# A recurrent scan, half of it moved into the projection loop; convolutions on VectorE and parked in DRAM

## The chip, the cores and the metric

The kernel runs on one core of one Trainium2 chip. The metric is device time in microseconds (us) of one execution. Engines are named as the profile names them: PE (TensorE matmul), DVE (VectorE), ACT (ScalarE), POOL (GpSimd), SP (SyncE, which here only issues DMAs).

## The reference

Two blocks on 512 tokens of width 2048. The change lies in the first one:

```python
h = rms_norm(x, norm_mix) @ w_in            # conv value+gate, r, k, v, three low-rank inputs
u = val * sigmoid(gate)                     # 1024 channels
u = silu(layer_norm(depthwise_conv(u, 31 taps, causal) + bias))
# RWKV-7 mixing, 16 heads of 64:
S = S * w_t + (S @ a_t) b_t + v_t k_t       # 64x64 state per head, one step per token
y_t = S @ r_t                               # then group norm per head, bonus, gate
x = x + concat(u, y) @ w_out                # then the expert layer (32 experts, 2 per token)
```

The second block (windowed attention, a state-space layer and a merge) follows; nothing in it changes. All values are float32; a projection is made of three matmuls on values split into a high and a low part.

## The kernel before

All that changes is in `phase_a` (L169 on): norm, projections, convolutions, scan, output projection. Channels lie on 128 partitions, the 512 tokens along the free axis.

A projection of 128 channels is one `dense`: four chunks of four weight tiles. Each chunk is loaded over the SP queue (L103), split by ACT (`wh`, L47) and DVE (`wl`, L48), and used by 12 matmuls (L111 to L113) against the split input `uh`, `ul`. Three buffers of split weights lie between the two. There are 43 such projections: 3 low-rank, 24 for r, k, v (three for each of 8 *pairs* of heads) and 16 for the 8 convolutions (gate and value).

The pair loop (`for p in range(8)`) makes r, k, v of a pair, the cumulated decay (a scan along the tokens, L410), operands scaled by it (`arr`, L427 to L433), the 64x64 score blocks of 8 chunks of 64 tokens (`sc`, L460), and more operands (L473 to L482), and writes them to DRAM (`dS`, `dL`). After pair 3 and after the loop, `inverse(0)` and `inverse(1)` read `dL` of four pairs and invert all their triangular blocks: a chain of 62 small dependent DVE instructions (L349, L351), then matmuls and copies (L340 on), and a last write to DRAM (`dX`, `dO`, L362). The scan proper (from L500) loads the inverses of both halves into `XB` and walks the 8 chunks, the two halves of heads by turns; a chunk is five *blocks* of eight 64x64 matmuls each (L561, L572, L579, L586, L594; the first and last chunk have four) with copies by ACT and adds by DVE between, each depending on the one before. After each second chunk `finish` (L524 on) normalises.

A convolution is a gate (`conv_gate`, two projections) and 31 taps (`conv_taps`): on DVE one instruction a tap (L303, L311), on Pool an ACT product (L308) and a Pool add (L309). `CONV` says which convolutions are made in which pair's turn; `FILL` those made after the loop. Here 0, 2 and 4 are in the loop; 1, 3, 5, 6, 7 after it; the first five of 0, 1, 2, 3, 4 on Pool, the rest on DVE. When all eight exist, the layer norm (L619 to L632) runs and then `w_out(0)`, the first half of the output projection; `w_out(1)` needs the scan's end.

The framework's scheduler puts the instructions of each engine in one fixed order, in which each engine then runs them; an instruction that waits holds up all that stand behind it on its engine.

Of the kernel before, what the change touches and what calls it, by code (L numbers as in the profile page):

```python
# [167 lines left out]
def phase_a(k):  # L168
# [22 lines left out]
    dS = tc.dram_tile([8, 128, 8, 2, 4, 64], F32, name="dS")  # L191
# [91 lines left out]
    def conv_gate(p, bufs):  # L283
# [4 lines left out]
        nc.gpsimd.tensor_mul(sgm, sgm, R)  # L288
# [6 lines left out]
    def conv_taps(p, ug):  # L295
        o = VEC["conv_dw"][0] + 31 * p
        cv[p] = co.tile([128, T], F32, name="cv%d" % p)
        pool = p in POOL
        b = vec(k, "conv_b", p)
        if pool:  # L300
            nc.scalar.activation(cv[p], ug[:, 0:T], AF.Identity, scale=k.vec[:, o:o + 1], bias=b)
        else:
            nc.vector.tensor_scalar(cv[p], ug[:, 0:T], k.vec[:, o:o + 1], b, op0=OP.mult, op1=OP.add)  # L303
        for j in range(1, 31):
            w = k.vec[:, o + j:o + j + 1]
            if pool:
# [3 lines left out]
            else:  # L310
                nc.vector.scalar_tensor_tensor(cv[p], ug[:, j:j + T], w, cv[p], op0=OP.mult, op1=OP.add)  # L311
# [81 lines left out]
    for p in range(8):  # L393
# [5 lines left out]
        arr = rp.tile([128, 8, 4, 64], F32, name="arr")  # L399
# [61 lines left out]
        for h, sc in enumerate(scs):  # L461
# [4 lines left out]
            nc.sync.dma_start(dS[:, 0:64, p, h, 1].rearrange("c q t -> q c t"), sc[0:64, :, 1])  # L466
            nc.sync.dma_start(dS[:, 64:128, p, h, 0:2].rearrange("c q a t -> q c a t"), sc[64:128])
            for i, b in ((2, 0), (3, 3)):
                nc.sync.dma_start(dS[:, 0:64, p, h, b].rearrange("c q t -> q c t"), arr[hr, :, i])
        for c0 in range(0, 8, 4):  # L470
# [28 lines left out]
    for g in range(2):  # L499
        for h in range(2):  # L500
            for i in range(2):
                q = slice(h * 64 + i * 32, h * 64 + i * 32 + 32)
                nc.sync.dma_start(XB[q, g * 32:(g + 1) * 32, i * 32:(i + 1) * 32],
                                  dX[g][i, h * 32:(h + 1) * 32].rearrange("m s t -> s m t"))
            q = slice(h * 64, h * 64 + 32)
            for o in range(0, 32, 16):
                nc.sync.dma_start(XB[q, g * 32 + o:g * 32 + o + 16, 32:64], dO[g][2 * h + o // 16])
    bp = sctx.enter_context(tc.tile_pool(name="bd", bufs=2, side=RIGHT))
    yp_ = sctx.enter_context(tc.tile_pool(name="yr", bufs=2, side=RIGHT))
    pc2 = bp.tile([64, 8, 2, 8], F32, name="pc2", bufs=1)  # L510
    for h in range(2):
        nc.sync.dma_start(pc2[:, :, h], pc[h * 64:(h + 1) * 64])

    def chunk(cc, g):

        bd = bp.tile([128, 4, 2, 5, 64], F32, name="bd", bufs=4)
        g4 = slice(4 * g, 4 * g + 4)
        lo_, hi = slice(0, 64), slice(64, 128)
        nc.scalar.dma_start(bd[hi, :, :, 0:4], dS[cc, hi, g4])
        nc.scalar.dma_start(bd[lo_, :, :, 0:3], dS[cc, lo_, g4, :, 0:3])  # L520
        nc.scalar.dma_start(bd[lo_, :, :, 4], dS[cc, lo_, g4, :, 3])
        return bd

    def finish(y, t):  # L524

        ts = slice(t * 128, (t + 1) * 128)
        for q in range(2):
            g4 = slice(4 * q, 4 * q + 4)
            yp = y[:, g4]
            pm = psr.tile([128, 4, 128], F32, name="pr")  # L530
            nc.tensor.matmul(pm, k.blk, yp, start=True, stop=True)
            nc.vector.scalar_tensor_tensor(yp, pm, -1.0 / 64, yp, op0=OP.mult, op1=OP.add)
            sq = yp_.tile([128, 4, 128], F32, name="fsq", bufs=1)
            nc.scalar.activation(sq, yp, AF.Square)
            pv = psr.tile([128, 4, 128], F32, name="pr")
            nc.tensor.matmul(pv, k.blk, sq, start=True, stop=True)
            nc.vector.tensor_scalar(sq, pv, 1.0 / 64, 64e-5, op0=OP.mult, op1=OP.add)
            rs = rsqrt(k, tmp, sq, [128, 4, 128])
            nc.vector.tensor_mul(yp, yp, rs)
            gt = yp_.tile([128, 4, 128], F32, name="fgt", bufs=1)  # L540
            nc.scalar.dma_start(gt, dG[g4, :, ts].rearrange("a q t -> q a t"))
            bon = yp_.tile([128, 4, 128], F32, name="fbon", bufs=1)
            nc.scalar.dma_start(bon, dB[g4, :, ts].rearrange("a q t -> q a t"))
            nc.gpsimd.tensor_mul(yp, yp, gt)
            nc.gpsimd.tensor_add(yp, yp, bon)
            nc.sync.dma_start(dY[:, g4, ts], yp)

    cur = [chunk(0, g) for g in range(2)]
    for cc in range(8):
        if cc % 2 == 0:  # L550
            y = yp_.tile([128, 8, 128], F32, name="y")
        for g in range(2):
            g4 = slice(4 * g, 4 * g + 4)
            bd = cur[g]
            nxt = chunk(cc + 1, g) if cc < 7 else None
            kq = slice(0 if cc else 64, 128)
            pq = psr.tile([128, 2, 4, 64], F32, name="pr")
            ys = y[:, g4, (cc % 2) * 64:(cc % 2 + 1) * 64]
            for i in range(4):
                for h in range(2):  # L560
                    nc.tensor.matmul(pq[h * 64:(h + 1) * 64, 0, i], bd[kq, i, h, 0], bd[kq, i, h, 3], start=True,  # L561
                                     stop=True)
            qs = bp.tile([128, 4, 64], F32, name="qs")
            nc.scalar.activation(qs, pq[:, 0], AF.Copy)
            state = bd[0:64, :, :, 3]
            if nxt and cc:
                nc.vector.tensor_mul(nxt[0:64, :, :, 3], state,
                                     pc2[:, g4, :, cc:cc + 1].to_broadcast([64, 4, 2, 64]))
            if cc:
                for i in range(4):  # L570
                    for h in range(2):
                        nc.tensor.matmul(pq[h * 64:(h + 1) * 64, 1, i], bd[0:64, i, h, 3], bd[0:64, i, h, 4],  # L572
                                         start=True, stop=True)
                nc.scalar.activation(ys, pq[:, 1], AF.Copy)
            pu = [psr.tile([64, 4, 64], F32, name="pr") for _ in range(2)]
            for i in range(4):
                for h in range(2):
# [1000 lines left out]
```

## Time and profile before

| | us |
|---|---|
| median of 3 runs | 3401.13 (3394.83 to 3404.06) |
| the profiled execution | 3402.26 |
| its span, first to last instruction | 3400.6 |
| last projection matmul before the layer norm | 692.5 |
| first layer-norm instruction (L624) | 746.9 |
| first matmul of `w_out(0)` / of `w_out(1)` | 773.2 / 891.4 |
| end of `phase_a`'s projections, expert layer starts | about 1008 |

Over the whole span PE is busy 93%, DVE 49%, ACT 31%, POOL 16%, and the mean granted clock is 0.963. An engine's row of a timeline reads: start, duration, engine, line, operation, output and inputs, and in square brackets the idle time before it and what ended it.

### The profile page before, as it was taken

The page shows a single profiled execution, that of the slowest core. Times are in us where ns is not written, and L with a number is a line of the kernel's source. Part 1 is how long each engine was busy: PE and PEld are TensorE (multiplying, and loading weights), DVE is VectorE, ACT ScalarE, POOL GpSimd, SP SyncE. Part 2 cuts the span into 40 slices and gives each one's busy share as a digit, 9 for nine tenths or more (in the row PEclk, how much of TensorE's full clock was granted, in tenths as well). Part 3 has the DMA queues.
Part 4 walks back from the last instruction along what each step waited for, and adds up shares of the span by engine and source line. Part 5 has one row for each costly group of instructions (what it writes and reads, how often), then busy time and mean ns, then how long its engine had stood idle before and what let it go on. Part 6 is the DMA issues. An engine that isn't in the chain of part 4 may idle for free.

```text
span 3400.6 us, 41331 instructions
## 1 busy us (share of the span) xinstructions
PE 3171.8 (93%) x15156; PEld 2156.7 (63%) x15157; DVE 1658.1 (49%) x3072; ACT 1052.2 (31%) x1793; POOL 546.0 (16%) x581
## 2 busy tenths in 40 slices
PE   8999998779989899898999898999999999999999
PEld 6777666547664333333333346778777878888887
DVE  6666667993332222232223238445799443344433
ACT  6464564344330000000000024363322242353322
POOL 3052254543210000000000005372000100000000
PEclk9999999789999999899999998999999999999999
DMA  4445444767668999998999965435332653334343
GB/s 149 129 122 139 125 121 123 139 131 181 219 239 352 420 420 414 406 407 349 419 420 411 404 249 167 143 144 166 134 106 104 203 183 118 124 130 137 133 146 118
DMA packets 352495, 743.47 MB, mean 219 GB/s; under 512 B 110688, under 2 KB 176608, under 8 KB 302112
## 3 DMA queue, kind: packets, MB, share of 16 engines
q1 hardware_dynamic: 272576, 650.24, 52.1%
q10 hardware_dynamic: 70624, 60.52, 7.2%
q0 software_dynamic: 9088, 30.03, 2.7%
q8 instruction: 121, 1.98, 0.2%
q14 instruction: 86, 0.70, 0.1%
HBM read 674.96 MB, written 73.01 MB: 220 GB/s over the span
## 4 chain that ended last, share of the span: by engine, by line
PE 46%; DMA 4%; POOL 2%; DVE 1%; issue 1%; ACT 0%; ACTq 0%; SPq 0%; DVEq 0%; POOLq 0%
PE pd L113 10%; PE pd L111 10%; PE pd L112 10%; PE pgate L916 3%; PE py L937 3%; PE pup L916 2%; DMA xg<-dTok,ix 1%; DMA w<-expert_w_gate_dram 1%; PE pb L946 1%; PE pb L947 1%; PE pb L815 1%; PE pr L1345 1%; POOL cn L1115 1%; PE ps L1296 0%; POOL cm L1114 0%
## 5 line engine op out<-in xcount | busy, mean ns | idle before, releaser
L48 DVE TENSOR_TENSOR wl<-wraw,wh 128x512 fp32r<-128x512 f32 x636 | 478.0, 754 | 496.0 <-ACT wh L47 487.1
L47 ACT ACTIVATE wh<-wraw 128x512 fp32r<-128x512 f32 x668 | 418.0, 628 | 834.0 <-PE pd L112 677.7
L113 PE MATMUL pd<-u2h,wl 128*128 128x512 f32 x1088 | 437.7, 402 | 10.2 <-DVE wl L48 10.1
L111 PE MATMUL pd<-u2h,wh 128*128 128x512 f32 x1088 | 439.4, 404 | 6.4 <-ACT wh L47 6.4
L112 PE MATMUL pd<-u2l,wh 128*128 128x512 f32 x1088 | 436.6, 401 | 0.0
L113 PE MATMUL pd<-uh,wl 128*128 128x512 f32 x688 | 282.6, 411 | 42.8 <-DVE wl L48 42.8
L916 PE MATMUL pgate<-w,xT 128*64 128x512 f32 x1024 | 305.6, 615 | 15.7 <-DMA w<-expert_w_gate_dram 15.0
L916 PE MATMUL pup<-w,xT 128*64 128x512 f32 x1024 | 293.5, 595 | 0.0
L111 PE MATMUL pd<-uh,wh 128*128 128x512 f32 x688 | 278.7, 406 | 12.0 <-ACT uh L220 7.2
L112 PE MATMUL pd<-ul,wh 128*128 128x512 f32 x688 | 278.1, 404 | 5.0 <-DVE ul L221 5.0
L113 PEld LDWEIGHTS pd<-u2h,wl 128*128 128x128 f32 x1088 | 206.5, 190 | 63.7 <-DVE wl L48 14.0
L309 POOL TENSOR_TENSOR cv<-cv,tap 128x512 f32<-128x512 f32 x150 | 227.6, 1517 | 105.1 <-ACT tap L308 92.4
L111 PEld LDWEIGHTS pd<-u2h,wh 128*128 128x128 f32 x1088 | 206.9, 190 | 56.7 <-ACT wh L47 9.0
L937 PE MATMUL py<-w,hidT 128*64 128x512 f32 x1024 | 236.0, 599 | 2.9 <-ACT hidT L929 2.9
L112 PEld LDWEIGHTS pd<-u2l,wh 128*128 128x128 f32 x1088 | 206.9, 190 | 47.8 <-issue 1.1
L948 DVE TENSOR_TENSOR hT<-hT,pb 128x512 f32<-128x512 f32 x256 | 159.2, 681 | 148.9 <-PE pb L947 148.9
L941 DVE SCALAR_TENSOR_TENSOR yl<-py,info,yh 128x512 fp32r<-128x512 f32 x64 | 48.0, 750 | 311.1 <-ACT yh L940 311.1
L916 PEld LDWEIGHTS pgate<-w,xT 128*64 128x64 f32 x1024 | 87.5, 142 | 170.0 <-issue 157.4
L113 PEld LDWEIGHTS pd<-uh,wl 128*128 128x128 f32 x688 | 134.0, 195 | 82.8 <-DVE wl L48 53.7
L916 PEld LDWEIGHTS pup<-w,xT 128*64 128x64 f32 x1024 | 87.0, 137 | 135.8 <-issue 133.6
L791 POOL DMA_INDIRECT xg<-dTok,ix x16 | 16.1, 1007 | 918.7 <-DVE info L798 908.3
L937 PEld LDWEIGHTS py<-w,hidT 128*64 128x64 f32 x1024 | 71.9, 137 | 143.8 <-issue 133.9
(566 smaller groups left out, 5054.8 us busy)
## 6 DMA issues: line engine op xcount, KB each, us to landing
w<-expert_w_gate_dram SPq DMA_DIRECT2D x128, 1024.0 KB, 14.7
w<-expert_w_up_dram SPq DMA_DIRECT2D x128, 1024.0 KB, 16.0
w<-expert_w_down_dram SPq DMA_DIRECT2D x128, 1024.0 KB, 14.0
wraw<-w_out_dram SPq DMA_DIRECT2D x128, 256.0 KB, 2.7
wraw<-w_rkv_dram SPq DMA_DIRECT2D x96, 256.0 KB, 3.0
wraw<-w_conv_dram SPq DMA_DIRECT2D x64, 256.0 KB, 3.5
wraw<-w_ga_dram SPq DMA_DIRECT2D x64, 256.0 KB, 2.6
wraw<-w_gs_dram SPq DMA_DIRECT2D x64, 256.0 KB, 2.6
```

The lines of the kernel that those rows point to most:

```text
L47: nc.scalar.activation(h, x, AF.Copy)
L48: (eng or nc.vector).tensor_sub(l, x, h)
L111: nc.tensor.matmul(ps, ah, bh, start=first, stop=False)
L112: nc.tensor.matmul(ps, ah, bl, start=False, stop=False)
L113: nc.tensor.matmul(ps, al, bh, start=False, stop=last)
L309: nc.gpsimd.tensor_add(cv[p], cv[p], pr)
L815: nc.tensor.transpose(ps[:, j, 0:m], xg[0:m, (j0 + j) * 128:(j0 + j + 1) * 128], k.ident[0:m, 0:m])
L916: nc.tensor.matmul(pgu[wi][q], xT[:, j0 + j, q], w[:, j * 512:(j + 1) * 512], start=j0 + j == 0, stop=j0 + j == KT - 1)
L937: nc.tensor.matmul(py[q], hidT[:, j, q], w[:, j * 512:(j + 1) * 512], start=j == 0, stop=j == 3)
L941: nc.vector.scalar_tensor_tensor(yl[nq], py[nq], info[nq, 0:1], yh[nq], op0=OP.mult, op1=OP.subtract)
L946: nc.tensor.matmul(ps, yh[nq, fs], og, start=True, stop=False)
L948: nc.vector.tensor_add(hT[:, f], hT[:, f], ps)
```

## The change

- `CONV` and `FILL`: convolutions 0, 2, 4, 5, 6 are made in the loop, only 1, 3, 7 after it. All taps are on DVE. The five are written to a DRAM tile `dC` and read back after the loop.
- A class `Half` holds the scan of four pairs. The one of pairs 0 to 3 is made after `inverse(0)`, and its `step(p - 4)` (two chunks and their `finish`) stands in the turn of pair p = 4 to 7. That of pairs 4 to 7 does its four steps after `inverse(1)`. The body of a step is that of the old chunk loop. `dS` is two DRAM tiles, `XB` is made for 32 and not 64 blocks, `arr` has one buffer and not two; each half has two `bd` buffers.
- The adds of squares of the norm, the gate product and the two last products of `finish` go from Pool to DVE; the 16 input tiles have a buffer each, and their squares and sums come after the low-rank matmuls.

```diff
-CONV = ((), (), (0,), (), (2,), (), (4,), ())
-FILL = (1, 3, 5, 6, 7)
-POOL = (0, 1, 2, 4, 3)
+CONV = ((), (5,), (0,), (), (2,), (6,), (4,), ())
+FILL = (1, 3, 7)
...
             for ps, (wh, wl) in zip(pl, ws):
                 mm3(nc, ps, wh[:, i % 4], wl[:, i % 4], uh[:, i], ul[:, i], i == 0, i == KT - 1)
+        for i, xt in enumerate(xs):
             if i:
-                sq = xp.tile([128, T], F32, name="xsq")
-                nc.scalar.activation(sq, xt, AF.Square)
-                nc.gpsimd.tensor_add(acc, acc, sq)
+                nc.scalar.activation(xt, xt, AF.Square)
+                nc.vector.tensor_add(acc, acc, xt)
...
-        nc.gpsimd.tensor_mul(sgm, sgm, R)
+        nc.vector.tensor_mul(sgm, sgm, R)
...
+        nc.vector.tensor_scalar(cv[p], ug[:, 0:T], k.vec[:, o:o + 1], b, op0=OP.mult, op1=OP.add)
         for j in range(1, 31):
             w = k.vec[:, o + j:o + j + 1]
-            if pool:
-                pr = cp1.tile([128, T], F32, name="tap")
-                nc.scalar.activation(pr, ug[:, j:j + T], AF.Copy, scale=w)
-                nc.gpsimd.tensor_add(cv[p], cv[p], pr)
-            else:
-                nc.vector.scalar_tensor_tensor(cv[p], ug[:, j:j + T], w, cv[p], op0=OP.mult, op1=OP.add)
+            nc.vector.scalar_tensor_tensor(cv[p], ug[:, j:j + T], w, cv[p], op0=OP.mult, op1=OP.add)
+        if early:
+            nc.sync.dma_start(dC[p], cv[p])
...
         if p == 3:
             inverse(0)
+            hctx = ExitStack()
+            half = Half(hctx, 0)
+        if p > 3:
+            half.step(p - 4)
         for i in CONV[p]:
             conv_taps(i, conv_gate(i, 1))
...
     last = inverse(1)
...
+    half = Half(sctx, 1)
+    for t in range(4):
+        half.step(t)
+    for p in sum(CONV, ()):
+        cv[p] = co.tile([128, T], F32, name="cv%d" % p)
+        nc.scalar.dma_start(cv[p], dC[p])
+    for p in FILL:
+        ug = conv_gate(p, len(FILL))
+        with tc.issue_after(last.ins):
+            conv_taps(p, ug)
```

What the scheduler makes of it is shown at three places. First DVE in the loop, from the projections of pair 3 on in the kernel before: `wl` is the split of a chunk, `sg`, `vv` and `arr` belong to the pair.

```order
L48 TENSOR_TENSOR wl_1483<-wraw_1480,wh_1482 128x512
L48 TENSOR_TENSOR wl_1650<-wraw_1647,wh_1649 128x512
L48 TENSOR_TENSOR wl_1668<-wraw_1665,wh_1667 128x512
L241 TENSOR_TENSOR sg_1498<-pd_1425,R_106 128x512
L48 TENSOR_TENSOR wl_1686<-wraw_1683,wh_1685 128x512
L244 SCALAR_TENSOR_TENSOR vv_1270<-sg_1498,vec_80,vv_1270 128x511
L410 SCALAR_TENSOR_TENSOR sg_1507<-resets_414,sg_1507 128x512
L433 TENSOR_TENSOR arr_1502<-rr_1269,pt_1514 128x8x64
```

And after the change, in the turn of pair 2 (`cv` is convolution 5):

```order
L47 TENSOR_TENSOR wl_1502<-wraw_1499,wh_1501 128x512
L304 SCALAR_TENSOR_TENSOR cv_1408<-ug_1405,vec_80,cv_1408 128x512 x3
L47 TENSOR_TENSOR wl_1525<-wraw_1522,wh_1524 128x512
L304 SCALAR_TENSOR_TENSOR cv_1408<-ug_1405,vec_80,cv_1408 128x512 x3
L47 TENSOR_TENSOR wl_1543<-wraw_1540,wh_1542 128x512
L304 SCALAR_TENSOR_TENSOR cv_1408<-ug_1405,vec_80,cv_1408 128x512 x2
L242 TENSOR_TENSOR sg_1517<-pd_1444,R_107 128x512
L304 SCALAR_TENSOR_TENSOR cv_1408<-ug_1405,vec_80,cv_1408 128x512
L47 TENSOR_TENSOR wl_1561<-wraw_1558,wh_1560 128x512
```

The taps now stand between the splits of the loop, two or three to a chunk.

Second, DVE around the end of the projections. Before (`it`, `X`: the chain of `inverse(1)`; `cv5`: a convolution of `FILL`):

```order
L48 TENSOR_TENSOR wl_6331<-wraw_6328,wh_6330 128x512
L349 TENSOR_TENSOR it_4437<-X_4421,L_4424 128x60
L351 TENSOR_TENSOR X_4421<-X_4421,it_4437 128x30x2
L349 TENSOR_TENSOR it_4437<-X_4421,L_4424 128x31
L351 TENSOR_TENSOR X_4421<-X_4421,it_4437 128x31
L292 TENSOR_TENSOR ug_6274<-pd_6201,sg_6197 128x512
L303 TENSOR_SCALAR cv5_6277<-ug_6274,vec_80 128x512
L48 TENSOR_TENSOR wl_6349<-wraw_6346,wh_6348 128x512
L311 SCALAR_TENSOR_TENSOR cv5_6277<-ug_6274,vec_80,cv5_6277 128x512 x3
L48 TENSOR_TENSOR wl_6367<-wraw_6364,wh_6366 128x512
L311 SCALAR_TENSOR_TENSOR cv5_6277<-ug_6274,vec_80,cv5_6277 128x512 x2
```

After the change, from the split before the last (`sc`: pair 6's last scores; `bd`: the state of step 2 of the first half):

```order
L47 TENSOR_TENSOR wl_6329<-wraw_6326,wh_6328 128x512
L47 TENSOR_TENSOR wl_6347<-wraw_6344,wh_6346 128x512
L542 TENSOR_TENSOR rr_3934<-pr_4213,vv_3935 128x512
L47 TENSOR_TENSOR hsl_4893<-sq_4889,hsh_4892 128x512
L553 SCALAR_TENSOR_TENSOR rr_3934<-rr_3934,vec_80,pr_4225 128x512
L565 TENSOR_TENSOR sc_4233<-pr_4235,upper_82 128x512
L565 TENSOR_TENSOR sc_4234<-pr_4236,upper_82 128x512
L565 TENSOR_TENSOR sc_4233<-pr_4247,upper_82 128x512
L565 TENSOR_TENSOR sc_4234<-pr_4248,upper_82 128x512
L578 TENSOR_TENSOR ak_4293<-arr_4167,pt_4179 128x512
L517 MEMSET pt_4881 128x8
L429 TENSOR_TENSOR bd_4312<-bd_4312,pr_4349 64x8x64
```

Before, the splits of the `FILL` projections stand among the inverse and the taps; now the last split `wl_6347` stands ahead of pair 6's last scores, and step 2, pair 7 (its scan at row 683 of the order, its last scores at row 709), the inverse (rows 716 to 788) and the taps of convolutions 1, 3, 7 (rows 789 to 888, with 17 instructions of the scan between) follow with no split between them. The layer norm stands at row 895.

Third, PE at the same place. Before, in the last `FILL` projections (`bd`: blocks of the scan):

```order
L111 MATMUL pd_6571<-uh_125,wh_6628 128x512
L112 MATMUL pd_6571<-ul_126,wh_6628 128x512
L586 MATMUL pr_4716<-bd_4585 64x64 x8
L594 MATMUL pr_4726<-bd_4585 64x64 x8
L561 MATMUL pr_4740<-bd_4632 64x64 x8
L113 MATMUL pd_6571<-uh_125,wl_6629 128x512
L111 MATMUL pd_6571<-uh_125,wh_6628 128x512
L112 MATMUL pd_6571<-ul_126,wh_6628 128x512
```

After the change, from the last projection matmul:

```order
L111 MATMUL pd_6289<-ul_127,wh_6346 128x512
L112 MATMUL pd_6289<-uh_126,wl_6347 128x512
L581 MATMUL pr_4295<-ident_58,ak_4293 128x128 x4
L585 MATMUL pr_4301<-ident_58,vv_3935 64x128 x4
L402 MATMUL pr_4316<-bd_3667 64x64 x8
L413 MATMUL pr_4316<-bd_3667 64x64 x8
L420 MATMUL pr_4337<-qs_4325,XB_2522 64x64 x4
L420 MATMUL pr_4338<-qs_4325,XB_2522 64x64 x4
L427 MATMUL pr_4349<-bd_3667 64x64 x8
L435 MATMUL pr_4359<-bd_3667 64x64 x8
```

Before, blocks of the scan stand between projection matmuls; now pair 6's last operands, step 2, pair 7 and all that follows stand behind the last of them, and the next big matmul is the first of `w_out(0)`. In `w_out(0)` and behind stand 204 of the scan's small matmuls and 8 of its statistics (L531, L538) before, 112 and 4 after.

## Rows read from the trace of the kernel before

**Rows 1.** Stretches: start:end, length, busy of each engine, granted clock, DMA share, GB/s.
```profile
0.00:50.00 50.00, 37.48 (x137) 27.69 (x139) 40.86 (x52) 30.74 (x52) 28.55 (x29) 0.97 0.57 181
50.00:527.00 477.00, 457.65 (x2131) 354.74 (x2130) 311.00 (x449) 271.12 (x411) 140.71 (x96) 0.99 0.47 126
527.00:594.00 67.00, 55.79 (x230) 43.26 (x231) 53.00 (x86) 28.82 (x43) 32.78 (x27) 0.93 0.49 119
594.00:747.00 153.00, 107.42 (x881) 80.49 (x880) 142.99 (x148) 58.49 (x106) 83.70 (x53) 0.83 0.70 139
747.00:774.00 27.00, 19.58 (x220) 12.20 (x221) 22.75 (x37) 17.12 (x33) 5.46 (x4) 0.91 0.68 140
774.00:891.00 117.00, 116.27 (x807) 90.92 (x806) 40.96 (x58) 41.18 (x77) 48.79 (x43) 0.98 0.61 168
```

**Rows 2.** Groups of instructions on DVE, 594 to 747 us: busy, mean ns, idle before.
```profile
L311 DVE SCALAR_TENSOR_TENSOR cv<-ug,vec,cv 128x512 f32<-128x512 f32 x90 | 101.0, 1122 | 2.0
L48 DVE TENSOR_TENSOR wl<-wraw,wh 128x512 fp32r<-128x512 f32 x14 | 20.4, 1463 | 4.7 <-ACT wh L47 4.7
```

**Rows 3.** One tile, the split weights, to 747 us: ns min/median/max, first and last start.
```profile
L48 DVE TENSOR_TENSOR wl<-wraw,wh x172: 672/691/1789, 6.6 to 685.5; 128x512 fp32r<-128x512 f32 x172
```

**Rows 4.** Timeline of DVE where Pool is idle, 725 to 728 us.
```profile
725.51 0.74 DVE L311 SCALAR_TENSOR_TENSOR cv<-ug,vec,cv 128x512 f32<-128x512 f32 x1
726.18 0.67 DVE L588 TENSOR_TENSOR bd<-bd,pr 64x512 f32<-64x512 f32 x1
726.77 0.67 DVE L154 TENSOR_TENSOR rs_y<-rs_y,rs_t 128x512 f32<-128x512 f32 x1
```

**Rows 5.** Groups on PE, 527 to 700 us.
```profile
L113 PE MATMUL pd<-uh,wl 128*128 128x512 f32 x128 | 57.2, 448 | 29.9 <-DVE wl L48 29.9
```

**Rows 6.** Timeline of PE at full clock, two projection matmuls in a row.
```profile
598.16 0.39 PE L111 MATMUL pd<-uh,wh 128*128 128x512 f32 x1
598.39 0.39 PE L112 MATMUL pd<-ul,wh 128*128 128x512 f32 x1
```

**Rows 7.** Timeline of PE: scan blocks at either clock (two records a matmul), and a statistic.
```profile
653.16 1.12 PE L561 MATMUL pr<-bd 64*64 64x64 f32 x16
718.29 0.69 PE L561 MATMUL pr<-bd 128*64 128x64 f32 x16
722.91 0.22 PE L586 MATMUL pr<-bd 128*64 128x64 f32 x1
857.18 1.12 PE L531 MATMUL pr<-y,blk 128*128 128x512 f32 x2
```

**Rows 8.** Groups on PE, 496 to 530 us: pair 7's own matmuls.
```profile
L457 PE MATMUL pr<-arr 64*128 64x128 f32 x32 | 2.9, 285 | 0.0
```

**Rows 9.** Groups by form, 0 to 1030 us, DVE at the start.
```profile
L221 DVE SCALAR_TENSOR_TENSOR ul<-xt,vec,uh 128x512 fp32r<-128x512 f32 x16 | 21.0, 1347 | 0.5 <-ACT uh L220 0.4
```

**Rows 10.** Timeline of DVE, pair 7 and the second inverse.
```profile
499.01 1.22 DVE L410 TENSOR_TENSOR_SCAN sg<-resets,sg 128x512 f32<-128x512 bf16 x1 [0.47 <-ACT sg L405]
526.43 1.29 DVE L460 TENSOR_TENSOR sc<-pr,upper 128x512 f32<-128x512 f32 x2
540.09 0.19 DVE L349 TENSOR_TENSOR it<-X,L 128x31 f32<-128x31 f32 x1 [2.32 <-DMA L<-dL]
```

**Rows 11.** One line, the inverse's chain: ns min/median/max, first and last start.
```profile
L349 DVE TENSOR_TENSOR it<-X,L x62: 192/375/1504, 282.1 to 592.8; 128x31 f32<-128x31 f32 x4, 128x60 f32<-128x60 f32 x4, 128x87 f32<-128x87 f32 x4, 128x112 f32<-128x112 f32 x4
```

**Rows 12.** Timeline: end of `inverse(0)`'s chain on DVE, then SP's issues.
```profile
318.73 0.21 DVE L351 TENSOR_TENSOR X<-X,it 128x31 f32<-128x31 f32 x1
346.54 0.33 SPq L362 DMA_DIRECT2D dO<-L  x1
637.38 2.59 SPq L507 DMA_DIRECT2D XB<-dO  x4
```

**Rows 13.** Timeline of DVE, the layer norm's start.
```profile
746.88 4.91 DVE L624 TENSOR_TENSOR cv<-cv,mean 128x512 f32<-128x512 f32 x8 [2.15 <-ACT mean L621]
```

**Rows 14.** Groups on PE, 890 to 1010 us.
```profile
L111 PE MATMUL pd<-wh,mixr_h 128*128 128x512 f32 x128 | 51.3, 408 | 5.3 <-ACT mixr_h L47 5.3
```

More of the change, by code (lines that the diff above doesn't have):

```diff
@@ L189, in phase_a @@
     nc.vector.tensor_scalar(oka, k.vec[:, o:o + 8], -1.0, 1.0, op0=OP.mult, op1=OP.add)
-    dS = tc.dram_tile([8, 128, 8, 2, 4, 64], F32, name="dS")
+    dS = [tc.dram_tile([8, 128, 4, 2, 4, 64], F32, name="dS%d" % g) for g in range(2)]
     dL = [tc.dram_tile([3, 2, 4, 8, 32, 32], F32, name="dL%d" % g) for g in range(2)]
@@ L213, in phase_a @@
     with ExitStack() as s:
-        xp = s.enter_context(tc.tile_pool(name="xin", bufs=4, side=RIGHT))
+        xp = s.enter_context(tc.tile_pool(name="xin", bufs=2, side=RIGHT))
         acc = xp.tile([128, T], F32, name="acc", bufs=1)
+        xs = []
         for i in range(KT):
-            xt = xp.tile([128, T], F32, name="xt")
+            xt = xp.tile([128, T], F32, name="xt", bufs=KT)
+            xs.append(xt)
             nc.sync.dma_start(xt, a["xT"][:, i])
@@ L498, in phase_a @@
     last = inverse(1)
[L499 to L577, printed above, removed]
-                    hr = slice(h * 64, (h + 1) * 64)
-                    nc.tensor.matmul(pu[h][:, i], XB[hr, (4 * g + i) * 8 + cc], qs[hr, i], start=True, stop=True)
-            for h in range(2):
-                nc.scalar.activation(state[:, :, h], pu[h], AF.Copy)
-            if nxt:
-                ptt = psr.tile([64, 4, 2, 64], F32, name="pr")
-                for i in range(4):
-                    for h in range(2):
-                        nc.tensor.matmul(ptt[:, i, h], bd[:, i, h, 2], bd[:, i, h, 3], start=True, stop=True)
-                if cc:
-                    nc.vector.tensor_add(nxt[0:64, :, :, 3], nxt[0:64, :, :, 3], ptt)
-                else:
-                    nc.vector.tensor_copy(nxt[0:64, :, :, 3], ptt)
-            py = psr.tile([128, 4, 64], F32, name="pr")
-            for i in range(4):
-                for h in range(2):
-                    nc.tensor.matmul(py[h * 64:(h + 1) * 64, i], bd[:, i, h, 3], bd[:, i, h, 1], start=True,
-                                     stop=True)
-            if cc:
-                nc.vector.tensor_add(ys, ys, py)
-            else:
-                nc.scalar.activation(ys, py, AF.Copy)
-            cur[g] = nxt
-        if cc % 2:
-            finish(y, cc // 2)
@@ L604, in phase_a @@
-    for i, p in enumerate(FILL):
-        ug = conv_gate(p, 4)
-        if p in POOL:
+    half = Half(sctx, 1)
[7 more added lines that the diff above has]
+        with tc.issue_after(last.ins):
             conv_taps(p, ug)
-        else:
-            with tc.issue_after(last.ins):
-                conv_taps(p, ug)
```

130 lines of the change are left out of this document (112 added, 18 removed).

## Prediction

> **What bounds the kernel now.** The first view read is the table of stretches [rows 1]; the reader is to compare PE's busy time with the stretch's length. Until 527 us PE is busy 495.1 of 527 us: 12.5 us idle in the first 50, 19.3 in the rest. PE sets the pace there. From 527 to 747 it is busy 163 of 220, and from 594 on DVE is busy 143 of 153: there DVE ends last, since the layer norm at 746.9 [rows 13] needs the last tap. In 774 to 891 (`w_out(0)`, with blocks of the scan among its matmuls) PE is busy 116.3 of 117. So the changed part has three regimes: a PE-bound loop, a stretch bound by DVE and dependent steps, and a PE-bound projection. What follows `phase_a` is not touched and starts when it ends, so a shift there passes to the end one for one.
>
> The second view is the groups of DVE in the middle stretch [rows 2]: 90 taps there take 1122 ns on average, 14 splits 1463, where the medians for the whole are 691 for a split [rows 3], and where Pool is idle a tap takes 0.74 and the next instruction starts 0.67 later (0.59 behind a two-operand one) [rows 4]. Pool at work beside DVE costs DVE here 90 x (1.12 - 0.74) = 35 us. That is what the change can win; what it can lose is order: before, PE still has 128/4 = 32 chunks to do at 527 us [rows 5], and they run beside pair 7's end, the inverse and the taps. The order after the change has none left to run there.
>
> **The sum** is made on the profiled execution (3402.26 us, 1.7 of them outside the span), which is 1.1 above the median.
>
> *1. When the last projection matmul runs.* PE's work until 527 us is 495.1 us [rows 1]. To it come the 32 chunks, 12 matmuls each, at a pitch of 0.23 [rows 6]: 88.3. Steps 0 and 1 of the first half are moved in: 4 + 5 + 5 + 5 = 19 blocks at 0.69 and 4 statistics at 1.1 [rows 7] are 17.5. Pair 7's own small matmuls, until 527 in that sum, now come later: 2.9 for the scores [rows 8] and about ten 512-wide ones at half a microsecond, with pair 6's last operands about 1 more: an estimate of -9.5. Together 591.4 us of work. Idle time: 31.9 before. At the start the 16 low parts took 1347 ns beside Pool [rows 9] against 0.74 alone; their excess of 9.7 us stood partly beside loads, of which I take 5 off. The 15 adds of squares, now on DVE, come behind the matmuls that wait; they cost 15 x 0.6 = 9 us at the loop's start at most, and I take them as hidden, since PE has a projection of the loop to do meanwhile. I add 3 for loads of weights that stand on SP behind the eight `XB` loads, which wait for `dO`, written 27.8 us after the inverse's chain ended [rows 12]. Bounds of that term: 0, or the 10 to 15 us at which four buffers of raw weights run dry. Idle 30; the last projection matmul ends at 591 + 30 = 621, against 692.5.
>
> This rests on taps that hide. DVE from 50 to 527 us is busy 311 of 477 [rows 1]. The five convolutions bring 5 x (30 x 0.665 + 0.6) = 103 us, steps 0 and 1 with their `finish` some 50 instructions at 0.6 or 30, the products 8 x 0.6 or 5; Pool's absence takes something off (35 us for 84 of Pool's work in the middle stretch, so at most 59 for the 141 here [rows 1]). 390 to 449 of some 500 us fits, but not evenly: a chunk with three taps costs DVE 0.69 + 3 x 0.67 = 2.7 and PE 12 x 0.23 = 2.8. Without that cover each convolution costs what DVE is over (a rival, below).
>
> *2. From there to the layer norm.* Now a series, nothing big on PE beside it. Step 2 of the first half: the two chunks chain at 722.9 + 0.2 - 718.3 = 4.8 [rows 7] and an add of 0.6 each, 11; one statistic and some five DVE instructions until pair 7's come through, 6: 17. Sigmoids and the decay's input, up to the scan L410: 5 (an estimate from three instructions of ACT and one of PE; bounds 2 and 8). From pair 7's decay scan to its last scores 526.43 + 1.29 - 499.01 = 28.7, of which 11 splits at 0.69 go: 21 [rows 10]. Scores to DRAM and back to the inverse's first instruction: 540.1 - 527.7 = 12.4 [rows 10]. DVE's order puts no tap in that gap, and nothing replaces it. The chain of the inverse: 62 x 0.375 = 23.3 [rows 11] with 11 instructions of step 3 between at 0.6: 30. The taps of 1, 3, 7: 93 x 0.665 = 62 [rows 4], and 17 instructions of the second half's scan between, 10: 72. The scan's first add stands in the row behind 65 of the taps, 43 us after the inverse; its chain needs `dO`, the `XB` loads of 2.6 and a chunk's 5, so 27.8 + 8 = 36 [rows 12]: no wait (5 at most, were the later write slower). The mean: 2. The sum is 17 + 5 + 21 + 12.4 + 30 + 72 + 2 = 159. Bounds: 141, where the transfer's last wait of 2.3 [rows 10], step 2's statistic (6), 3 of the sigmoids and step 3's 6.6 in the inverse's chain vanish; 175, where the sigmoids take 3 more, the scan's operands 5, and some 18 blocks run at the lower clock level of 1.2 GHz, 1.12 instead of 0.69 [rows 7] (the granted clock is 0.83 of full in the stretch before, a mean of both levels [rows 1]). The layer norm starts at 621 + 159 = 780, 33 later than 746.9 [rows 13].
>
> *3. From there to the end of `phase_a`.* The layer norm itself has no change. In `w_out(0)` and behind stand 204 - 112 = 92 scan matmuls fewer, 11.5 blocks at 0.69 = 8, and 4 statistics at 1.1 = 4; as PE is full there [rows 1], all of it counts: -12. The wait for `mixr_h` of 5.3 [rows 14] shrinks as the scan ends earlier relative to `w_out(0)`; I take -2. Bounds of both: -18 and -6. The five read-backs of `dC` (0.26 MB each, on ACT's queue) have the whole tail to land: 0. Writing `dC` costs SP five issues in the loop: 0, at worst 2.
>
> *Sum*: +33 - 14 = +19; 3402.3 + 19 = **3421 us**.
>
> **A rule against the change.** The rows say that DVE is not full in the loop (311 of 477 us [rows 1]), while in single chunks with taps it is at PE's pace. The Trainium skill, page "Perfetto Trace Analysis", section "Optimizing Scalar/DVE Operations", says that where DVE is saturated it may pay to move work from it to ScalarE or even GpSimd; the change moves 155 tap steps the other way. By that rule the outcome would be rival B, about 3446; by the rows' average, 3421.
>
> **The rivals.**
> *A, faster: the tail is as short as DVE's work, and the loop loses its stalls.* For it: the excess of 35 us beside Pool; and PE's largest idle from 527 on is for the split (29.9 [rows 5]). If the loop's 19.3 us of idle are all of that kind, they go: 591 + 8 = 599. With the tail at its lower bound, 141, the layer norm starts at 740, 7 sooner; with -14 to -18 behind it the end is 21 to 25 sooner: 3379. It decides when the first L631 (the old L624) starts before 751. Against it: in most of the loop DVE was not beside Pool's taps (141 of 477 us), and the 12.4 us transfer and pair 7's chain hold no Pool work.
> *B, slower: DVE paces the loop.* For it: the tap chunk at 2.7 against 2.8 us, to which a pair's own some forty instructions come; DVE runs in order, so a tap that waits for its gate delays a split. If each of the five convolutions leaves 5 us uncovered, +25: 3446. Against it: three buffers of split weights and the tenth to fifth of DVE's time that is free.
> *C: weights late behind the `XB` loads on SP*, 10 to 15 instead of 3: 3431. For it: their place in SP's row; against it: four raw buffers ahead.
> *D, no change: the idle time is only moved.* PE's idle from 527 to 774 was 64 us and in the loop 32; if the tail runs 10 us shorter than summed and the loop saves 8, both within the bounds, it ends at 3403. For it: every handover in the tail was measured beside a full PE queue, so a tail with PE free may run faster.
>
> **How the numbers follow.** A run of this kernel can be told from no change by about 0.3%, 10 us. Chances: the forecast 0.42 (own range 3412 to 3436), A 0.18, B 0.14, C 0.06, D 0.20. Faster by over 10 us is A, 0.18; within 10 us is D and the lowest edge of the forecast, 0.22; slower the rest, 0.60. The range takes in the upper half of A and most of B, 3388 to 3448.
>
> **What would show it.** (1) The last `pd<-uh,wl` of the projections at 621: at 600 the loop lost its stalls (A), at 640 and with idle time ended by `wl` in chunks with taps, B; idle ended by DMA `wraw` behind the `XB` loads, C. (2) Taps at 0.74 and a pitch of 0.67 everywhere. (3) From there to the layer norm 159 us with PE busy under a third and no tap in the 12 us ahead of the inverse. (4) The first `w_out(0)` matmul at about 806, that of `w_out(1)` some 14 us closer to it. (5) The expert layer and the second block as long as before. The prediction is wrong if the tail is far from 159, or if the loop waits where it did not.

## The result and the profile after

The changed kernel takes 3419.51 us (median of 5 runs, 3414.01 to 3423.68) against 3399.43 for the kernel before beside it: ratio 1.0058, 95% interval 1.0042 to 1.0075, about 20 us slower. The forecast was 3421. Its profiled execution spans 3417.8 us against 3400.6.

The stretches of the changed kernel, columns as in [rows 1], cut at 50 us, the last projection matmul, the layer norm's start, the first matmul of `w_out(0)` and the end of the output projection:

```profile
0.00:50.00 50.00, 41.91 (x167) 32.96 (x169) 40.01 (x73) 34.96 (x57) 4.28 (x14) 1.00 0.58 193
50.00:597.00 547.00, 543.02 (x2741) 428.36 (x2740) 392.30 (x644) 232.85 (x358) 4.86 (x7) 0.99 0.53 137
597.00:779.00 182.00, 86.39 (x682) 62.37 (x681) 122.13 (x222) 37.41 (x63) 6.04 (x8) 0.60 0.50 105
779.00:804.00 25.00, 18.78 (x203) 11.39 (x202) 17.50 (x30) 15.33 (x28) 0.00 (x0) 0.95 0.55 102
804.00:1025.00 221.00, 214.14 (x1076) 162.62 (x1076) 73.95 (x108) 73.43 (x141) 46.01 (x48) 0.98 0.65 208
```

Read PE's idle time, length less busy. Ahead of `w_out(0)` it was 96 us before (12.5, 19.4, then 11.2 + 45.6 + 7.4 [rows 1]) and is 114 now: 8.1 + 4.0 in the loop, where DVE is busy 392 of 547 us, but 95.6 + 6.2 behind it. The loop gave 20 us, the stretch behind it took 38. The granted clock in the 182 us to the layer norm is 0.60 of full, a mean of PE's two levels.

The split and the taps, which answer to [rows 2, 3]. The first row is from the view of the tile `wl`, the second from the view of the taps' line (shortest, median and longest in ns):

```profile
L47 DVE TENSOR_TENSOR wl<-wraw,wh x172: 676/689/698, 6.8 to 581.3; 128x512 fp32r<-128x512 f32 x172
```

```profile
L304 DVE SCALAR_TENSOR_TENSOR cv<-ug,vec,cv x240: 727/747/759, 152.3 to 771.8; 128x512 f32<-128x512 f32 x120
```

The longest split is 698 ns, where it was 1789; no tap is over 759.

The series behind the loop, in DVE's timeline of the changed kernel: pair 7's decay scan, its last scores, the inverse's first and last instruction, the last tap, the layer norm (they answer to [rows 10, 13]).

```profile
621.57 1.23 DVE L515 TENSOR_TENSOR_SCAN sg<-resets,sg 128x512 f32<-128x512 bf16 x1 [1.31 <-ACT sg L510]
...
645.87 0.69 DVE L565 TENSOR_TENSOR sc<-pr,upper 128x512 f32<-128x512 f32 x1 [0.33 <-PE pr L562]
...
667.13 0.19 DVE L344 TENSOR_TENSOR it<-X,L 128x31 f32<-128x31 f32 x1 [1.66 <-DMA L<-dL]
...
698.69 0.21 DVE L346 TENSOR_TENSOR X<-X,it 128x31 f32<-128x31 f32 x1
...
771.85 0.74 DVE L304 SCALAR_TENSOR_TENSOR cv<-ug,vec,cv 128x512 f32<-128x512 f32 x1
...
778.94 3.70 DVE L631 TENSOR_TENSOR cv<-cv,mean 128x512 f32<-128x512 f32 x6 [1.39 <-ACT mean L628]
```

`w_out(0)` starts at 803.6 (773.2 before), `w_out(1)` at 912.5 (891.4). From there to the end of the execution all kernels below need 2497 to 2509 us, with the same work. So the start of `w_out(1)` tells what a variant is worth, to within 13 us.

### The profile page after: what moved, and what is told of

Read it like the earlier page. It is cut to its first block, busy times and chain, and to the rows that moved or that the text cites. A ratio compares the mean times of both kernels' runs of the same rounds, so it can differ in the third digit from the quotient of the medians.

```text
span 3417.8 us, 41091 instructions
## 1 busy us (share of the span) xinstructions
PE 3168.8 (93%) x15156; PEld 2162.0 (63%) x15157; DVE 1656.8 (48%) x3266; ACT 959.8 (28%) x1641; POOL 260.4 (8%) x393
## 4 chain that ended last, share of the span: by engine, by line
PE 46%; DMA 4%; POOL 2%; DVE 1%; issue 1%; ACT 0%; SPq 0%; ACTq 0%; DVEq 0%; POOLq 0%
PE pd L112 10%; PE pd L110 10%; PE pd L111 10%; PE pgate L922 3%; PE py L943 3%; PE pup L922 2%; DMA xg<-dTok,ix 1%; DMA w<-expert_w_gate_dram 1%; PE pb L952 1%; PE pb L953 1%; POOL cn L1121 1%; DMA yt<-dY 1%; PE pb L821 1%; PE pr L1351 1%; POOL cm L1120 0%
## 5 line engine op out<-in xcount | busy, mean ns | idle before, releaser
L47 DVE TENSOR_TENSOR wl<-wraw,wh 128x512 fp32r<-128x512 f32 x636 | 442.5, 698 | 479.0 <-ACT wh L46 465.6
L112 PE MATMUL pd<-u2h,wl 128*128 128x512 f32 x1088 | 437.0, 402 | 12.3 <-DVE wl L47 12.1
L110 PE MATMUL pd<-uh,wh 128*128 128x512 f32 x688 | 271.2, 395 | 10.8 <-ACT uh L221 7.5
L112 PE MATMUL pd<-uh,wl 128*128 128x512 f32 x688 | 272.9, 397 | 1.3 <-DVE wl L47 1.2
L304 DVE SCALAR_TENSOR_TENSOR cv<-ug,vec,cv 128x512 f32<-128x512 f32 x240 | 172.5, 748 | 1.6
L110 PEld LDWEIGHTS pd<-uh,wh 128*128 128x128 f32 x688 | 130.4, 189 | 41.2 <-ACT uh L221 7.2
```

The costliest lines, as they stand in the source:

```text
L47: (eng or nc.vector).tensor_sub(l, x, h)
L110: nc.tensor.matmul(ps, ah, bh, start=first, stop=False)
L112: nc.tensor.matmul(ps, al, bh, start=False, stop=last)
```

## The experiments

"Us against before" is the ratio to the runs of before on the same chip, less one, times 3400. The other times are those of the trace, in us.

| kernel | pair 7's decay scan | layer norm | `w_out(1)` | ratio, interval | us against before |
|---|---|---|---|---|---|
| before | 499.0 | 746.9 | 891.4 | | |
| changed | 621.6 | 778.9 | 912.5 | 1.0058, 1.0042 to 1.0075 | +20 |
| e1: steps behind the loop | 522.8 | 704.9 | 888.3 | 0.9983, 0.9973 to 0.9994 | -6 |
| e2: before, no Pool taps | 485.4 | 744.5 | 866.5 | 0.9896, 0.9875 to 0.9917 | -35 |
| e3: projections of 1, 3, 7 late | 586.2 | 758.5 | 892.7 | 1.0007, 0.9997 to 1.0016 | +2 |
| e4: two `arr` | 619.8 | 778.7 | 910.5 | 1.0066, 1.0047 to 1.0086 | +22 |
| e5: five convolutions behind | 589.7 | 851.0 | 963.9 | 1.0211, 1.0192 to 1.0230 | +72 |
| e6: e2, 5 and 6 in the loop | 520.2 | 682.7 | 853.4 | 0.9871, 0.9854 to 0.9887 | -44 |
| e7: e2, 5 in the loop | 512.1 | 708.0 | 850.7 | 0.9865, 0.9849 to 0.9882 | -46 |
| e8: taps free of the inverse | 619.7 | 746.7 | 950.4 | 1.0156, 1.0139 to 1.0173 | +53 |
| e9: e7, new start | 506.1 | 701.7 | 853.4 | 0.9897, 0.9880 to 0.9913 | -35 |
| e10: PSUM divided | 609.1 | 766.7 | 909.1 | 1.0057, 1.0040 to 1.0073 | +19 |
| e11: halves by turns, by steps | 511.2 | 688.8 | 890.1 | 0.9985, 0.9976 to 0.9995 | -5 |
| e12: halves by turns, by chunks | 511.8 | 692.1 | 865.9 | 0.9924, 0.9906 to 0.9941 | -26 |

**What Pool cost: e2.** Of the kernel before only this is changed:

```diff
-POOL = (0, 1, 2, 4, 3)
+POOL = ()
```

> The kernel before with all taps on DVE (five convolutions moved from Pool), nothing else changed. Theory P: the loop's idle PE time (19.3 us in 50 to 527) was Pool's work slowing DVE: it falls to about 5, as in the changed kernel, and taps take 0.74 everywhere. In the middle stretch DVE gets two convolutions more (41 us) and loses the 35 us of excess: time 3385 to 3395. Rival: the loop's idle time went in the changed kernel because more other work (two more convolutions, the scan) fills it; here it stays near 19, the middle stretch is longer, and the time is 3400 to 3415.

Its stretches:

```profile
50.00:527.00 477.00, 476.63 (x2254) 375.46 (x2253) 335.77 (x552) 219.98 (x330) 9.77 (x10) 0.99 0.50 133
527.00:597.00 70.00, 68.32 (x319) 56.74 (x318) 62.84 (x128) 21.46 (x31) 8.98 (x8) 0.95 0.60 147
```

Theory P holds for the loop: PE idles 0.4 us in 50 to 527, 19.4 before. The time falls by 35 us, more than either range allowed. The layer norm starts 2 us sooner only, but `w_out(1)` 25: in `w_out(0)` and behind, 8 of the scan's small matmuls are left, where 204 stood before. The other 10 us or so lie behind `w_out(1)`, where nothing was changed and the traces differ by up to 13, so 25 is what the trace shows for this part. It wins alone, and the rest of the change has to lose more than it.

**What the steps in the loop cost: e1, e3, e10, e4.** e1 takes the four steps out:

```diff
-        if p > 3:
-            half.step(p - 4)
...
+    for t in range(4):
+        half.step(t)
     hctx.close()
```

> The changed kernel with the four steps of the first half of the scan taken out of the loop and put behind it (all else as changed; the result is the same). Theory O (order): the changed kernel loses 39 us of PE time between the last projection matmul and the layer norm because no projection is left to run beside pair 7, the inverse and the taps, and it is the steps in the loop that let the projections of 1, 3, 7 run ahead of pairs 5 to 7. Without them 22 of these 24 chunks (61 us of PE) stand behind pair 7's lora matmul again: pair 7's decay scan at about 535 instead of 621.6, layer norm at 705 to 725 instead of 779, some 17 us of scan blocks more behind it: 3365 to 3385. Rival L (length): pair 7, inverse and taps are a series on DVE and its waits, whatever PE does beside: layer norm at 765 to 780 and the scan's 17 us on top: 3420 to 3440.

The layer norm came at 704.9, 74 us sooner, as theory O said. The time of 3391 did not follow (forecast 3365 to 3385): 25 of the 74 us are lost before `w_out(0)` and 25 more in it. PE's timeline of e1 inside the layer norm shows where:

```profile
727.59 1.12 PE L402 MATMUL pr<-bd 64*64 64x64 f32 x16 [3.69 <-DMA bd<-dS]
731.36 3.78 PE L634 MATMUL pd<-lsq,ones 128*128 128x512 f32 x4 [2.65 <-ACT lsq L633]
739.05 1.19 PE L420 MATMUL pr<-qs,XB 64*64 64x64 f32 x8 [3.90 <-DMA XB<-dO]
740.17 2.07 PE L634 MATMUL pd<-lsq,ones 128*128 128x512 f32 x2
```

The norm's statistic (L634) stands among scan blocks that wait for loads; the norm takes 50 us instead of 25.

e3 leaves the steps where they are and orders the late projections behind pair 7's lora matmul:

```diff
-        ug = conv_gate(p, len(FILL))
+        with tc.issue_after(lora.ins):
+            ug = conv_gate(p, len(FILL))
```

> The changed kernel with the projections of convolutions 1, 3, 7 ordered on PE behind pair 7's lora matmul. Theory O: pairs 6 and 7 come about 35 us sooner (decay scan of pair 7 at about 586), the 24 chunks run beside pair 7's scores, the inverse and the taps, whose splits cost DVE 16 us: layer norm at about 760, 3400 in all. PE idles ahead of pair 7 instead. Rival L: the layer norm stays at 779 or later, 3419 or more.

As theory O said: the decay scan at 586.2 for 586, the layer norm 1.5 us ahead of the 760 forecast, the time 3399. With 24 chunks back beside the series, 18 us of the 20 are regained; rival L is out.

e10 asked why the steps let the projections run ahead of pairs 5 to 7. Pairs and steps take their buffers of PSUM (where PE writes its results) from one pool of four.

```diff
-    psr = keep.enter_context(tc.tile_pool(name="psr", bufs=4, space=PSUM))
+    psr = keep.enter_context(tc.tile_pool(name="psr", bufs=2, space=PSUM))
...
-                pq = psr.tile([128, 2, 4, 64], F32, name="pr")
+                pq = psr.tile([128, 2, 4, 64], F32, name="ph", bufs=2)
```

(and so for the other tiles of a step.)

> The changed kernel with the four PSUM buffers that pairs and steps share divided: two for the pairs, two for the steps. Theory B (buffers): in the changed kernel a pair's first small matmul needs a buffer that a step's result holds, so pairs 4 and 5 are 95 us apart (decay scans 368.4 and 463.3) and the projections of 1, 3, 7 run ahead meanwhile; with buffers of its own pair 5 follows after 60 to 75 us, some 10 chunks stand behind pair 7's lora matmul, and the time is 3400 to 3412, although two buffers for the pairs also slow pairs 1 to 4. Rival R: the distance is set by other things (the one arr buffer, the step's own waits, the in-order engines): 90 us or more between pairs 4 and 5, 3418 or more.

The decay scans of pairs 4 and 5, on DVE:

```profile
399.22 1.22 DVE L515 TENSOR_TENSOR_SCAN sg<-resets,sg 128x512 f32<-128x512 bf16 x1
465.09 1.22 DVE L515 TENSOR_TENSOR_SCAN sg<-resets,sg 128x512 f32<-128x512 bf16 x1 [0.88 <-ACT sg L510]
```

They are 66 us apart instead of 95, but not because pair 5 comes sooner: in the changed kernel the two scans are at 368.4 and 463.3, so pair 4 is 31 us later here and pair 5 2 us later. Sooner come only pairs 6 and 7, by 13 and 12 us, and of 12 us at the layer norm 3 are left at `w_out(1)` and none in the time. So the run doesn't show that the shared buffers hold pair 5 back. PE idles 4 us only in the changed kernel's loop, so the distance lies in the scheduler's order; what in the steps sets it stays open.

e4 gave `arr` its second buffer (`bufs=1` taken off, one buffer of the parked convolutions less).

> The changed kernel with two buffers of arr instead of one (paid by one buffer less of convolution results); the order of instructions is the same. Theory O: the one buffer holds up nothing that counts, pair 7's first arr product waits for its decay scan: layer norm at 779 and 3419, within 4. Rival B: pairs wait for the reads of the one arr buffer, so pairs 5 to 7 come closer together, the last projection matmul stays at 597 but pair 7 is 5 to 15 us sooner: 3404 to 3414.

No change (layer norm 778.7): theory O.

**Convolutions and taps: e5, e8, e6, e7.**

```diff
-CONV = ((), (5,), (0,), (), (2,), (6,), (4,), ())
-FILL = (1, 3, 7)
+CONV = ((), (), (0,), (), (2,), (), (4,), ())
+FILL = (1, 3, 5, 6, 7)
...
-        ug = conv_gate(p, len(FILL))
+        ug = conv_gate(p, 4)
```

The second edit gives the five gate products four buffers, as in the kernel before.

> The changed kernel with the convolutions divided as before: 0, 2, 4 in the loop, five (1, 3, 5, 6, 7) after it; steps in the loop and DVE for all taps stay. With the steps out of the loop the run of before without Pool took 3363, so this run shows what steps in the loop cost beside five convolutions. Theory O: as beside three (29 us), for 16 of the 40 chunks still stand behind pair 7: 3385 to 3400. Rival T (taps): 155 taps, 103 us, now lie behind the inverse, which ends where it did: layer norm at 785 to 800 instead of 779, 3420 to 3435.

Rival T, and worse than it (layer norm 851.0, not 785 to 800). The last projection ends at 681.8, and the fifth gate product stands behind taps, at 805.5, as it needs a buffer that they release. So 155 taps and the scan follow one another. Five buffers were not tried.

e8 drops `with tc.issue_after(last.ins):` around the taps of the changed kernel.

> The changed kernel without the rule that the taps of 1, 3, 7 stand behind the inverse on DVE; the scheduler mixes them into the inverse's chain. Theory O: the two are one series on DVE (32 + 74 us) whichever comes first, so the layer norm stays at 779 within 5 or comes a little sooner by what the chain waits between its instructions, and the scan's second half comes later: 3413 to 3424. Rival: the chain leaves gaps and the waits for the operands of the scan vanish from the tail: layer norm 10 to 20 us sooner, 3398 to 3410.

Both were wrong. The layer norm comes 32 us sooner than in the changed kernel, the time is 33 us longer. The stretch ahead of `w_out(1)` and its first matmul (stretches, then PE's timeline) show the reason:

```profile
890.00:952.00 62.00, 34.96 (x347) 24.02 (x346) 22.47 (x36) 12.54 (x28) 0.64 (x4) 0.70 0.50 118
```

```profile
950.36 0.79 PE L110 MATMUL pd<-wh,mixr_h 128*128 128x512 f32 x1 [8.96 <-ACT mixr_h L46]
```

The taps pushed the inverse's end from 699 to 759, and the scan's second half, which needs it, ran on alone behind `w_out(0)`: PE idles 27 of these 62 us and at the end waits 9 for the scan's last result (`mixr_h`). So there is a second limit, the scan's end. From the inverse's end to `w_out(1)` it is 191 us here and 214 in the changed kernel, which waits 1.1 us there.

e6 and e7 change `CONV` and `FILL` of e2: 5 and 6, or 5 alone, go into the loop.

> The kernel before with all taps on DVE and with convolutions 5 and 6 made in the loop (their results stay in memory, no parking), only 1, 3, 7 after it; the scan stays behind the loop with its halves by turns. Theory V: in the run of before without Pool DVE was busy 123 of 147 us between the last projection and the layer norm, so two convolutions fewer there (41 us) bring the layer norm from 744 to about 710 to 720; 10 to 15 us are given back in the first half of the output projection, where scan blocks move: 3345 to 3355. Rival S: the scan and its waits end last there, the layer norm's statistic stands behind its matmuls on PE as with the steps behind the loop (50 instead of 25 us): 3360 to 3375.

> As the run before it with only convolution 5 moved into the loop, four after it. Theory V: half of the gain, 3350 to 3358. Rival S: 3360 to 3370.

The layer norm came 62 and 37 us sooner than in e2, `w_out(1)` 13 and 16. By the ratios the time is 9 and 11 us less, but their intervals overlap that of e2. The rest is the second limit: in e6 `w_out(1)` waits 9.9 us for the scan, and ahead of it PE idles 14 of 53 us:

```profile
800.00:853.00 53.00, 38.62 (x382) 29.39 (x380) 18.60 (x29) 16.33 (x34) 16.21 (x13) 0.93 0.49 148
```

e6 and e7 have the lowest medians of all, 3355.4 and 3355.6 us: theory V's range for e7, a hair above it for e6, although e6's layer norm at 683 came well ahead of the 710 forecast.

**What else separates the change from e6: e9, e11, e12.** e9 adds to e7 the new start (the diff of the input loop) and the gate product on DVE.

> The run of before without Pool and with convolution 5 in the loop, and in addition the change's new start: 16 input buffers, squares and their sums behind the low-rank matmuls and on DVE, the gate product on DVE. My term for the start was 5 us less idle time; the changed kernel showed 8.1 instead of 12.5 idle in the first 50. Expected: 3355 less 4 to 5, 3348 to 3353. Rival: the sums on DVE come in the loop's way and nothing is left of it: 3354 to 3360.

The rival: nothing is gained. PE idles 7.9 us in the first 50 instead of 11.3, and 1.6 instead of 0.0 to 527; the layer norm is 6 us sooner than in e7, `w_out(1)` 3 us later. By ratio e9 is 11 us slower, but the two intervals touch (0.9880 and 0.9882), and the traces show no cause for it.

e11 and e12 put the whole scan of the changed kernel behind `inverse(1)`. The edit of e11:

```diff
-            hctx = ExitStack()
-            half = Half(hctx, 0)
-        if p > 3:
-            half.step(p - 4)
...
-    half = Half(sctx, 1)
+    halves = [Half(sctx, g) for g in range(2)]
     for t in range(4):
-        half.step(t)
+        for half in halves:
+            half.step(t)
```

> The changed kernel with the whole scan behind the second inverse and its halves stepping by turns (half 0, half 1, half 0, ...), as in the kernel before; the three convolutions behind the loop, the parking in DRAM, the new start and DVE for all products of the change stay. It stands between the run with the steps put behind the loop one half after the other (6 us under before) and the run of before without Pool with convolutions 5 and 6 in the loop (44 under). Theory T (turns): one half's chain leaves PE waiting, two halves by turns fill each other's waits, so nearly all of the 38 us between those two runs is won: 3353 to 3366. Rival M: it is not the turns but the rest that differs (the parking and reading back, the start, the sums and products on DVE, one buffer of arr): 3375 to 3395.

> As the run before, but the halves take turns chunk by chunk (and both finish after each second chunk), as in the kernel before; there they took turns by steps of two chunks, and its trace showed the halves' statistics some 30 us apart each and the wait of the second output projection for the scan's end. Theory T2: turns by chunk let the two chains fill each other's waits; the scan's end and with it the second output projection come 25 to 35 us sooner: 3357 to 3368. Rival M: single buffers of a half (its y, its qs, the shared ones of the finish) and the rest of the change hold it all the same: 3380 to 3395.

In e11 theory T fell: 3392.6 us, within rival M's range. In e12 each half does one chunk, then the other. It is 21 us faster by the ratios (3370.8, between its two ranges), and `w_out(1)` starts 24 sooner. So walking the halves by turns matters, but chunk by chunk. The 18 us that still part it from e6 are open (buffers of a half, the parking, products on DVE).

Read in a row, these runs split the 64 us between the changed kernel and e6: 25 for half the scan in the loop (changed to e11), 21 for turns by steps and not by chunks (e11 to e12), 18 open. Each was taken off with the others as they stood.

## Why the prediction was right, and where two steps cancelled

The total was right within 2 us, and so was the mechanism in outline: the projections run out, then comes a series with PE idle, and it costs more than the loop gives. Two terms of the sum were not right, and that the layer norm still came within 1 us of the forecast is luck: one was 24 us too much, the other 23 too little, for reasons that have nothing to do with each other. By its own signs the prediction failed in part: the tail took 182 us, outside its bounds of 141 to 175, with PE busy 86 of them, not under a third, and 597 for the last projection was its sign of rival A.

| term | forecast | measured |
|---|---|---|
| last projection matmul ends | 621 | 597.2 |
| of it PE idle | 30 | 12.1 |
| to pair 7's decay scan | 22 | 24.4 |
| to its last scores | 21 | 25.0 |
| to the inverse | 12.4 | 20.6 |
| the inverse | 30 | 31.8 |
| the taps | 72 | 73.7 |
| the mean | 2 | 6.3 |
| layer norm starts | +33 | +32.1 |
| from there on | -14 | -15 |

*Step 1, idle time.* I carried over the loop's idle 19 us. They were the doing of Pool's taps (e2: 0.4 left), which I had given to rival A; PE's work was 585, not 591. Rival A was right on the loop and wrong on the tail. The 3 us that I had added for weights behind the `XB` loads were right: they are most of the 4.0 us of idle that the loop has left. The timelines of SP, ACT and PE:

```profile
382.59 3.14 SPq L376 DMA_DIRECT2D XB<-dO  x2
...
387.22 2.00 SPq L102 DMA_DIRECT2D wraw<-w_rkv_dram  x4
...
392.54 0.63 ACT L46 ACTIVATE wh<-wraw 128x512 fp32r<-128x512 f32 x1 [6.47 <-DMA wraw<-w_rkv_dram]
...
393.22 0.50 PE L110 MATMUL pd<-uh,wh 128*128 128x512 f32 x1 [2.97 <-ACT wh L46]
```

This is rival C's wait, at the forecast's size and not at the rival's 10 to 15. Of rival B there is 0.9 us of idle behind a split. DVE had room, 392 busy of 547 us. So the rule of the Trainium skill ("Perfetto Trace Analysis", "Optimizing Scalar/DVE Operations") had no case here. The Trainium skill's page "SBUF — State Buffer", section "Who interferes with whom", says that VectorE and GpSimd share a pair of ports under an exclusive lock. e2 agrees with it: a split takes 697 ns on average where it took 807. Groups on DVE, 50 to 527 us, of before and of e2:

```profile
L48 DVE TENSOR_TENSOR wl<-wraw,wh 128x512 fp32r<-128x512 f32 x130 | 104.6, 807 | 91.9 <-ACT wh L47 87.8 <-PE pr L340 2.4 <-PE pd L112 1.7
L48 DVE TENSOR_TENSOR wl<-wraw,wh 128x512 fp32r<-128x512 f32 x137 | 95.1, 697 | 57.4 <-ACT wh L47 50.6 <-DMA wraw<-w_rkv_dram 3.4 <-PE pd L113 3.3
```

*Step 2, the series.* Its order was right, its length 182, not 159. The largest miss is the transfer before the inverse. On SP the last `dL` write is issued at 651.3. The load of `L` stands on ACT; ACT's timeline, and the row of DVE's at the same moment:

```profile
658.03 0.60 ACT L582 ACTIVATE g<-pr 128x512 f32<-128x512 f32 x1 [3.34 <-DMA dS<-g]
658.65 0.59 ACT L587 ACTIVATE g<-pr 64x512 f32<-64x512 f32 x1
663.20 0.34 ACTq L317 DMA_DIRECT2D L<-dL  x1
663.59 0.38 ACT L405 ACTIVATE qs<-pr 128x256 f32<-128x256 f32 x1 [4.34 <-DMA dS<-g]
...
663.59 1.29 DVE L293 TENSOR_TENSOR ug<-pd,sg 128x512 f32<-128x512 f32 x2 [6.77 <-DMA dS<-g]
```

The load now stands behind the copies of pair 7's second group (L582, L587), which wait for their one buffer; before, it was issued at 535.3, ahead of them. I had counted instructions on DVE and not read ACT's order. But that is half of it: the copies end at 659.2, and the load waits 4 us more. The profile puts the end of that wait, and of DVE's for the first late gate products, to the landing of a write of pair 7's `g` to `dS`. The tiles of the inverse and the late gate products are taken where the pair loop's pools have been closed, so they may wait for that memory. This is read from trace and program and was not tried apart.

The mean took 6.3 us and not 2. On PE its matmuls (L626) run from 773.7 to 778.3, behind blocks of the scan, five of the eight after the last tap:

```profile
773.15 0.63 PE L420 MATMUL pr<-qs,XB 64*64 64x64 f32 x15
773.71 4.56 PE L626 MATMUL pd<-cv,ones 128*128 128x512 f32 x10
```

Two waits for transfers that I had put at 0 were there (groups on PE, 597 to 779 us), but off the path. They can have cost the layer norm 1.1 us at most, the time from the last tap's end at 772.6 to the mean's matmuls:

```profile
L420 PE MATMUL pr<-qs,XB 64*64 64x64 f32 x112 | 9.8, 275 | 11.2 <-DMA XB<-dO 11.2
L626 PE MATMUL pd<-cv,ones 128*128 128x512 f32 x16 | 8.6, 672 | 4.4 <-DMA cv<-dC 4.2 <-DVE cv L304 0.2
```

The read-backs of `dC` held up the first mean matmul until 670.2, a hundred us ahead of the last tap; the `XB` loads are waited for 11.2 us, under the taps.

*Step 3* nearly held: -15 for -14. But I had expected all of it by `w_out(1)`, and there it is -11; the other -4 lies where the traces differ by up to 13 with the same work.

Not foreseen at all: that taking the cover back wins little by itself, since the scan's end stands right behind the layer norm as a limit (e1, e6, e8).

## What to carry to other kernels

Before moving work into a full loop, read from the order what then stands beside the serial part behind it: here PE idles 20 us less in the loop and 38 more behind it, where no projection was left to run. A part of a change that wins alone (no Pool taps beside DVE, 35 us) can be hidden by one that loses, so time the parts. When a total comes out right, check its terms: here misses of 24 and 23 us hid each other. And when one end is brought forward, look for the next: a layer norm 62 us sooner was worth some 10.

## What the runs showed of the hardware

With Pool's taps (a product on ACT and an add on Pool each) beside it, DVE is late although it is busy 311 of 477 us only [rows 1]. Stretches of the kernel before, columns as in [rows 1]:

```profile
234.00:258.00 24.00, 18.80 (x72) 13.87 (x72) 22.16 (x21) 15.51 (x25) 18.78 (x13) 0.93 0.29 77
336.00:371.00 35.00, 28.04 (x117) 20.48 (x117) 20.80 (x20) 23.46 (x37) 26.87 (x18) 0.90 0.30 83
448.00:474.00 26.00, 21.83 (x105) 15.75 (x103) 25.09 (x23) 16.30 (x27) 19.60 (x14) 1.00 0.34 97
474.00:500.00 26.00, 26.00 (x123) 20.53 (x121) 13.57 (x18) 19.93 (x31) 24.18 (x17) 1.00 0.59 148
```

16 of the loop's 19.4 us of idle lie in the first three, where Pool works and a pair's products stand on DVE between the splits; in the fourth Pool is as busy, DVE is not, and PE idles nothing. DVE and PE around the longest of these waits:

```profile
451.93 1.78 DVE L48 TENSOR_TENSOR wl<-wraw,wh 128x512 fp32r<-128x512 f32 x1
453.63 1.77 DVE L428 TENSOR_TENSOR kkr<-kkr,av 128x512 f32<-128x512 f32 x1
455.44 1.66 DVE L429 TENSOR_TENSOR arr<-kkr,ip 128x512 f32<-128x512 f32 x1
457.03 1.48 DVE L430 TENSOR_SCALAR av<-av,vec,oka 128x512 f32<-128x512 f32 x1
458.43 1.75 DVE L48 TENSOR_TENSOR wl<-wraw,wh 128x512 fp32r<-128x512 f32 x1
...
460.23 0.50 PE L113 MATMUL pd<-uh,wl 128*128 128x512 f32 x1 [3.45 <-DVE wl L48]
```

So it is not the split's own length alone (1.75 us here, 0.69 at the median [rows 3]) that makes PE wait, but a run of five slow instructions, the split last. 12.6 us of the idle time end with a split on DVE; the rest ends mostly with ACT, which has Pool's products among its own work. e2 takes the adds and the products away together, so the runs don't part the two.
